# Two-part transformer model: the index scores of the second token tile computed between the two halves of the query projection, and two 64-wide norm rows loaded by another engine

## The chip, the core and the metric

One Trainium2 chip, one core. The metric is the device time of one execution in microseconds (us), taken over several runs. TensorE (PE) multiplies and transposes, VectorE (DVE) and ScalarE (ACT) work on elements, GpSimd (POOL) does a few element operations, SyncE (SP) issues most DMAs.

## The reference

A sequence of 256 tokens with 1024 features passes through two parts. The first part has a sparse-attention layer (layer A), an MLP, a layer with compressed keys and values (layer B) and another MLP. A second part follows. The change is in layer A, which opens the program:

```python
proj = rms_norm(x, a_attn_norm) @ w_in
q = rms_norm(proj[..., :1024].reshape(b, s, 16, 64), q_gain)
k = rms_norm(proj[..., 1024:1088], k_gain)           # one key head
v = proj[..., 1088:1152]
qi, ki, wi = index queries (8 x 64), index key (64), index weights (8)
dots  = einsum('bqhd,bsd->bqhs', qi, ki) * 64 ** -0.5
score = einsum('bqh,bqhs->bqs', wi * 8 ** -0.5, relu(dots))
score = where(admiss, score, NEG)                    # chunks of 64 keys
_, idx = top_k(score, 64)
logits = q @ k[idx] * 64 ** -0.5 + rel_bias[t5_bucket(idx - t)]
h = x + softmax(logits) @ v[idx] @ a_w_o
h = h + relu(rms_norm(h) @ up) ** 2 @ down
```

## The kernel before

Tokens lie in two tiles of 128 partitions (tile 0 and tile 1). Tile 0 sees 128 keys, tile 1 all 256 (`SK`). Everything is fp32 and each product is made of three matmuls: activations and weights are split into a high and a low part. For weights `wsplit` (lines 240 to 263) loads a raw piece through SP (L247, L249), ScalarE writes the high part `whi` (L252, or L260 with a gain), VectorE the low part `wlo` (L255, or L261 with a gain); `mm_tok` (L275, L276, L278) then multiplies. There are 3 raw buffers and 4 buffers of high and low parts. PSUM has 2 `acc` tiles for projections, 2 `tr` for transposes, 3 `lg` for dots and logits, 1 `po` for attention outputs.

A tile scheduler takes the instructions in the order in which the program writes them, models the time of each, and fixes from that one order for each engine. At run time an engine works through its fixed list and never skips an instruction that waits. `keep_in_program_order` (used by `ldk`, L453) pins an instruction where the program writes it. `behind(hold)` asks the scheduler to place what is in it after the instruction `hold`.

Layer A (`layer_a`, from L573) runs so:

- The two halves of tile 0 of `x` are loaded by SP at the head of the program (L146, L148). The attention norm's gain goes to columns. The first key/value/index weights are loaded (L247, four quarters), then tile 1 of `x` (L584). `bcast_row` (L137) loads `gk` and `gq`, the 64-wide key and query norm gains, broadcast to 128 partitions, by DMAs that POOL issues. `norm_x` squares and sums (L175), transposes (L165) and splits the activations into `axh`, `axl`. `gkq` (L593) is the product of the two gains; it is first used when the keys are normed.
- The keys, values, index queries, index keys and index weights come out of two weight chunks of 356 columns (`kvi`).
- `scores(t)` (L630 to L646): four dots on PE (L485, output `lg`), each followed by a ReLU on ACT (L640, `rl`) and two multiply-adds on DVE (L644, `scr`), a chain over 8 index heads.
- `topk(t)` (L648 to L659): eight rounds of MAX (L653) and MATCH_REPLACE (L655) on DVE, a chain too, then the mask `madd` (L658).
- A half `i` of the query projection is a `dense` with `ev_q` (L665 to L675): ACT copies and squares (L668, L669), DVE sums the squares (L671) and computes a factor (L156), POOL scales (L674). `q_T` (L677) transposes the result.
- Attention steps (`att_step`, L533 to L568), two heads each, 16 in all, in a skewed pipeline: `f1` makes logits (L485) and adds the mask `madd` with a matmul by the identity (L487), DVE adds the bias and finds the extremum (L553), ACT takes exponentials (L493); `f2` transposes the probabilities and copies them (L502 on DVE, or ACT); `f3` multiplies with the values (L509). After each four steps `a_done` divides by the sum: `o` (L697) on DVE, then four transposes (L165) and a split into `aoh`, `aol` (L169).
- `out_proj` multiplies with `a_w_o`, whose first two weight chunks are held behind the two masks.

The order of the parts is written out in `PLAN_A` (L28) and played by `weave` (L519): `s` scores, `k` top-k, `q` a half of the query projection, `t10` transposes of tile 1's half 0, `*n` n rounds of the attention pipeline, `**` all that are left.

```python
for f in plan.split():
    if f == "**":
        for _ in rounds: pass
    elif f[0] == "*":
        for _ in range(int(f[1:] or 1)): next(rounds, None)
    else:
        items[f]()
```

Of the kernel before, what the change touches and what calls it, by code (L numbers as in the profile page):

```python
# [24 lines left out]
NACC, NTR, NLG, NPO = 2, 2, 3, 1  # L25


PLAN_A = "s0 k0 q0 q1 t00 t01 s1 * t10 k1 *4 t11 **"  # L28
PLAN_B = "k0 q0 k2 20 q1 k1 30 21 *2 q2 31 * 22 k3 q3 *2 32 *4 23 *2 o00 33 *5 o10 *2 o01 o11"
PLAN_C = "ck mg ms cq q0 mw k0 mn v0 v1 ml B0 *2 q1 *3 B1 *3 o0 k1 *3 k2 * v2 * q2 B2 o1 *2 a0 *2 a1 * b1 * p0 p1 *4 b0 *3"  # L30

# [58 lines left out]
def block_kernel(ctx: ExitStack, tc: tile.TileContext, a, out: bass.AP):  # L90
# [11 lines left out]
    def nm(s):  # L102
        uid[0] += 1
        return f"{s}_{uid[0]}"
# [16 lines left out]
    def sm(s, cols=8):  # L121
        w, n = SMALL.get(s, (8, 2))
        return sp.tile([P, w], F32, tag="s_" + s, name=nm(s), bufs=n)
# [13 lines left out]
    def bcast_row(dst, src_1d, n):  # L137
        G.dma_start(dst, row(src_1d, n))

    def row(src_1d, n):  # L140
        return bass.AP(tensor=src_1d.tensor, offset=src_1d.offset, ap=[[0, P], [1, n]])
# [29 lines left out]
    def rms_stats(h):  # L171
        ss2 = sm("ss2", 2)
        for i in range(2):
            j = tj("sq")
            A.activation(j, h[:, i * 512:(i + 1) * 512], AF.Square, accum_out=ss2[:, i:i + 1])  # L175
        ss = sm("ss", 1)
        V.tensor_tensor(ss[:, :1], ss2[:, 0:1], ss2[:, 1:2], op=OP.add)
        return rsqrt_eps(ss[:, :1], 1.0 / D, 1)

    def norm_T(h, r, gain, x, t):  # L180

        if r is not None or gain is not None:
            hns = t4("hn")
        for i in range(2):
            c = slice(i * 512, (i + 1) * 512)
            hn = h[:, c] if r is None and gain is None else hns[:, c]
            if gain is None:
                if r is not None:
                    V.tensor_scalar(hn, h[:, c], r, None, op0=OP.mult)
            elif r is None:  # L190
                V.tensor_tensor(hn, h[:, c], gain[:, c], op=OP.mult)
            else:
                V.scalar_tensor_tensor(hn, h[:, c], r, gain[:, c], op0=OP.mult, op1=OP.mult)
            ps = transposes(hn, 4)
            put(x, i, t, ps.rearrange("p (k n) -> p k n", k=4))
# [3 lines left out]
    @contextmanager  # L199
    def behind(ins):  # L200

        with ExitStack() as st:
            for i in ins or ():
                st.enter_context(tc.issue_after(i.ins))
            yield

    def norm_x(x, gain, fold=True):


        holds, rs = [tuple(mark[1:])], []  # L210
        for t in range(2):
            if fold:
                rs.append(rms_stats(hres[t]))
                norm_T(hres[t], None, gain, x, t)
            else:
                norm_T(hres[t], rms_stats(hres[t]), gain, x, t)
            holds.append(tuple(mark))
        return holds, rs

    def xpair(s, kt=8):  # L220

        if kt == 2:
            b = t4(s, F32R).rearrange("p (e k n) -> p e k n", e=2, k=2)
            return [b[:, 0]], [b[:, 1]]

        def part(sfx):
            return [t4(s + sfx, F32R, n * 256).rearrange("p (k n) -> p k n", k=n)
                    for n in (min(4, kt - g) for g in range(0, kt, 4))]
        return part("h"), part("l")
# [70 lines left out]
    def out_proj(x, w, scale=None, holds=(None, None)):  # L300
        dense_by_tile([(x, 8, w, 512 * ci, 512, None, lambda t, ps, ci=ci: add_res(t, ci, ps, scale))
                       for ci in range(2)], holds)
# [150 lines left out]
    def ldk(dst, src):  # L453
        tc.keep_in_program_order(nc.sync.dma_start(dst, src))
# [70 lines left out]
    def weave(plan, items, steps):  # L525

        rounds = stages(steps)
        for f in plan.split():
            if f == "**":
                for _ in rounds:  # L530
                    pass
            elif f[0] == "*":
                for _ in range(int(f[1:] or 1)):  # L533
                    next(rounds, None)
            else:
                items[f]()
        assert next(rounds, rounds) is rounds
# [36 lines left out]
    def layer_a():  # L574
# [7 lines left out]
        V.tensor_copy(gcol, gp[:, :8])  # L582
        wkv = [wparts(w, 8, *kvc[0], gain=gcol, by_k=True)]
        nc.sync.dma_start(hres[1], a["x"][0, P:2 * P, :])  # L584
        gk = sm("gk", 64)
        gq = sm("gq", 64)
        bcast_row(gk[:, :64], a["a_k_norm"][0], 64)
        bcast_row(gq[:, :64], a["a_q_norm"][0], 64)
        gkq = sm("gkq", 64)
        x = xpair("ax")  # L590
        holds, rs = norm_x(x, None)
        with behind(holds[2]):
            V.scalar_tensor_tensor(gkq[:, :64], gk[:, :64], 0.125, gq[:, :64], op0=OP.mult, op1=OP.mult)  # L593
        kvi = [t4("kvi") for _ in range(2)]
# [82 lines left out]
        def q_T(t, ci):  # L677
            tp = transposes(qn[t, ci], 4)
            A.activation(qT[t][:, ci * 512:(ci + 1) * 512], tp, AF.Copy)
# [22 lines left out]
        for i in range(2):  # L702
# [3 lines left out]
            for ci in range(2):  # L706
                items["t%d%d" % (i, ci)] = lambda i=i, ci=ci: q_T(i, ci)
        weave(PLAN_A, items, steps)
        out_proj(oT, a["a_w_o"][0], holds=picked)
# [570 lines left out]
    def final():  # L1280
        g = gain_row(a["norm_final_g_2"])
        for t in range(2):
# [7 lines left out]
            for i in range(2):  # L1290
                nc.sync.dma_start(out[0, t * P:(t + 1) * P, i * 512:(i + 1) * 512], gh[i])

    layer_a()
    mlp(0)
    layer_b()
# [30 lines left out]
```

## Time and profile before

| what | value |
|---|---|
| median of 3 runs | 1154.01 us (1153.26 to 1154.15) |
| the profiled execution, its own time | 1153.44 us |
| its span in the trace | 1151.3 us |
| mean granted TensorE clock | 0.998 |
| weights and other data moved | 191.92 MB, mean 167 GB/s |

The span runs from the first to the last recorded instruction. The profiled execution's own time is 2.1 us longer than its span. An engine's busy time is the union of its instructions. The idle time in front of an instruction is given in square brackets with what ended it.

### The profile page before, as it was taken

How to read it: one execution, taken by the hardware profiler on the slowest of the kernel's cores; microseconds unless marked ns; L12 is line 12 of the kernel's file. 1: busy time of each engine (PE TensorE's matmuls, PEld its weight loads, DVE VectorE, ACT ScalarE, POOL GpSimd, SP SyncE). 2: the span in 40 equal slices, each digit the busy share in tenths (PEclk: the TensorE clock that was granted, in tenths of full speed). 3: DMA queues.
4: the chain of work that ended last, by engine and by line, in shares of the span. 5: the costliest groups of instructions: out<-in, count | busy, mean ns of one | idle time of the engine just before them, and what ended most of it. 6: DMA issues, size and time to landing. Idle time of an engine off the chain costs nothing.

```text
span 1151.3 us, 17271 instructions
## 1 busy us (share of the span) xinstructions
PE 1124.7 (98%) x6912; PEld 992.4 (86%) x6912; DVE 678.6 (59%) x1224; ACT 614.1 (53%) x1070; POOL 68.4 (6%) x80
## 2 busy tenths in 40 slices
PE   7989999999998999999999999999999999999997
PEld 6767898889897879989989999888888878999996
DVE  6794754445688574554366976645475566544544
ACT  7654555445487555554446664555554435433443
POOL 1210000000043000000000000010000030000000
PEclk9999999999999999999999999999999999999999
DMA  9540646554462346565538444744544535546641
GB/s 282 199 147 23 216 151 222 182 184 132 132 212 75 104 147 214 170 219 184 171 107 281 147 147 148 240 143 147 183 147 153 183 122 178 206 154 213 202 141 61
DMA packets 105383, 191.92 MB, mean 167 GB/s; under 512 B 6616, under 2 KB 22960, under 8 KB 105304
## 3 DMA queue, kind: packets, MB, share of 16 engines
q1 hardware_dynamic: 104056, 187.16, 48.6%
q0 software_dynamic: 1040, 3.54, 1.0%
q8 instruction: 54, 0.88, 0.3%
q14 instruction: 25, 0.20, 0.1%
q10 hardware_dynamic: 208, 0.13, 0.0%
HBM read 189.68 MB, written 1.13 MB: 166 GB/s over the span
## 4 chain that ended last, share of the span: by engine, by line
PE 92%; DVE 4%; ACT 1%; issue 1%; DMA 0%; POOL 0%; SPq 0%; POOLq 0%; DVEq 0%; ACTq 0%
PE acc L275 10%; PE acc L276 10%; PE acc L278 9%; PE dn L361 7%; PE dn L362 7%; PE dn L364 7%; PE up L310 5%; PE up L313 5%; PE up L311 5%; PE tr L165 3%; PE po L509 2%; PE qk L310 2%; PE qk L311 2%; PE lg L485 2%; PE qk L313 2%; PE fp L310 1%
## 5 line engine op out<-in xcount | busy, mean ns | idle before, releaser
L255 DVE TENSOR_TENSOR wlo<-raw,whi 128x1024 fp32r<-128x1024 f32 (+3 forms) x340 | 385.5, 1177 | 211.3 <-ACT whi L252 211.1
L252 ACT ACTIVATE whi<-raw 128x1024 fp32r<-128x1024 f32 (+3 forms) x340 | 322.9, 1007 | 212.3 <-PE dn L364 86.7
L310 PE MATMUL up<-mxh,whi 128*128 128x256 f32 x448 | 110.9, 281 | 0.0
L311 PE MATMUL up<-mxl,whi 128*128 128x256 f32 x448 | 110.7, 280 | 0.0
L361 PE MATMUL dn<-whi,uh 128*128 128x512 f32 x256 | 100.7, 395 | 0.0
L362 PE MATMUL dn<-wlo,uh 128*128 128x512 f32 x256 | 100.6, 394 | 0.0
L158 POOL TENSOR_TENSOR rr<-rv,mhalf 128x1 f32<-128x1 f32 (+2 forms) x42 | 39.8, 950 | 821.5 <-DVE rv L156 806.2
L310 PEld LDWEIGHTS up<-mxh,whi 128*128 128x128 f32 x448 | 84.3, 188 | 0.7
L311 PEld LDWEIGHTS up<-mxl,whi 128*128 128x128 f32 x448 | 84.2, 188 | 0.7
L275 PE MATMUL acc<-whi,cxh 128*128 128x512 f32 (+1 forms) x192 | 74.5, 389 | 0.0
L276 PE MATMUL acc<-wlo,cxh 128*128 128x512 f32 (+1 forms) x192 | 72.3, 378 | 0.0
L313 PE MATMUL up<-mxh,wlo 128*128 128x256 f32 x448 | 71.0, 280 | 0.0
L364 PE MATMUL dn<-whi,ul 128*128 128x512 f32 x256 | 69.5, 394 | 0.0
L313 PEld LDWEIGHTS up<-mxh,wlo 128*128 128x128 f32 x448 | 60.3, 188 | 0.0
L361 PEld LDWEIGHTS dn<-whi,uh 128*128 128x128 f32 x256 | 48.1, 188 | 13.2 <-ACT whi L252 2.6
L364 PEld LDWEIGHTS dn<-whi,ul 128*128 128x128 f32 x256 | 48.1, 188 | 11.2
L362 PEld LDWEIGHTS dn<-wlo,uh 128*128 128x128 f32 x256 | 48.1, 188 | 10.6
L278 PE MATMUL acc<-whi,cxl 128*128 128x512 f32 (+1 forms) x192 | 50.6, 382 | 0.0
L169 DVE TENSOR_TENSOR ul<-sq,uh 128x512 fp32r<-128x512 f32 x28 | 19.4, 692 | 51.8 <-ACT uh L169 51.5
L310 PE MATMUL qk<-cxh,whi 128*128 128x256 f32 x192 | 49.1, 287 | 0.0
L311 PE MATMUL qk<-cxl,whi 128*128 128x256 f32 x192 | 48.2, 282 | 0.0
L493 ACT ACTIVATE lg<-lg,nx 128x128 f32<-128x128 f32 (+1 forms) x80 | 35.4, 446 | 16.3 <-DVE nx L553 16.3
(414 smaller groups left out, 2410.2 us busy)
## 6 DMA issues: line engine op xcount, KB each, us to landing
raw<-in_w_in SPq DMA_DIRECT2D x38, 1024.0 KB, 5.2
raw<-in_mlp_w_up SPq DMA_DIRECT2D x32, 1024.0 KB, 5.3
raw<-in_mlp_w_down SPq DMA_DIRECT2D x32, 1024.0 KB, 5.1
raw<-in_w_gate SPq DMA_DIRECT2D x10, 1024.0 KB, 5.5
raw<-in_w_up SPq DMA_DIRECT2D x10, 1024.0 KB, 5.1
raw<-in_w_down SPq DMA_DIRECT2D x10, 1024.0 KB, 5.0
raw<-in_w_in SPq DMA_DIRECT2D x6, 688.0 KB
raw<-in_a_w_in SPq DMA_DIRECT2D x4, 1024.0 KB
```

The lines of the kernel that those rows point to most:

```text
L158: G.tensor_tensor(r[:, :n], v[:, :n], mhalf[:, :n], op=OP.pow)
L252: A.activation(hi[:, c], raw[:, c], AF.Copy)
L255: V.tensor_tensor(lo[:, c], raw[:, c], hi[:, c].bitcast(F32), op=OP.subtract)
L275: PE.matmul(o, s0, wh[:, k, :], start=(g + k == 0), stop=False)
L276: PE.matmul(o, s0, wl[:, k, :], start=False, stop=False)
L278: PE.matmul(o, xs(xl, g + k, t), wh[:, k, :], start=False, stop=(g + k == KT - 1))
L310: PE.matmul(o, s0, xh[(g + k) // 4][:, (g + k) % 4, :], start=(g + k == 0), stop=False)
L311: PE.matmul(o, s0, xl[(g + k) // 4][:, (g + k) % 4, :], start=False, stop=False)
L313: PE.matmul(o, wl[:, k, col:col + P], xh[(g + k) // 4][:, (g + k) % 4, :], start=False, stop=(g + k == KT - 1))
L361: PE.matmul(ps, s0, wh[:, k, :], start=(c == 0 and k == 0), stop=False)
L362: PE.matmul(ps, s0, wl[:, k, :], start=False, stop=False)
L364: PE.matmul(ps, xs(u[1], k, t), wh[:, k, :], start=False, stop=(c == nc_ - 1 and k == kt - 1))
```

## The change

Two edits. In `PLAN_A` the item `s1` (scores of tile 1) moves from behind the query transposes `t00 t01` to between `q0` and `q1`. In `layer_a` the rows `gk` and `gq` are allocated and loaded behind `norm_x` instead of ahead of it, and by SP (`ldk`, pinned in program order) instead of POOL (`bcast_row`).

```diff
-PLAN_A = "s0 k0 q0 q1 t00 t01 s1 * t10 k1 *4 t11 **"
+PLAN_A = "s0 k0 q0 s1 q1 t00 t01 * t10 k1 *4 t11 **"
...
         nc.sync.dma_start(hres[1], a["x"][0, P:2 * P, :])
-        gk = sm("gk", 64)
-        gq = sm("gq", 64)
-        bcast_row(gk[:, :64], a["a_k_norm"][0], 64)
-        bcast_row(gq[:, :64], a["a_q_norm"][0], 64)
         gkq = sm("gkq", 64)
         x = xpair("ax")
         holds, rs = norm_x(x, None)
+        gk = sm("gk", 64)
+        gq = sm("gq", 64)
+        ldk(gk[:, :64], row(a["a_k_norm"][0], 64))
+        ldk(gq[:, :64], row(a["a_q_norm"][0], 64))
         with behind(holds[2]):
             V.scalar_tensor_tensor(gkq[:, :64], gk[:, :64], 0.125, gq[:, :64], op0=OP.mult, op1=OP.mult)
```

On SP, at the head of the program, between the load of tile 1 of `x` and the second chunk of key/value weights (`raw_180`):

```order
 L247 DMA raw_105<-in_a_w_in 128x4x356
 L584 DMA h_71<-in_x 128x1024
+L454 DMA gk_173<-in_a_k_norm 128x64
+L454 DMA gq_174<-in_a_q_norm 128x64
 L247 DMA raw_180<-in_a_w_in 128x4x356
 L441 DMA oh_317<-in_c_oh 33x512
```

The two small loads now stand ahead of the second weight chunk on SP; POOL's list loses them.

On VectorE, where tile 0's top-k ends (`scr_389` is tile 0's working array, `scr_390` tile 1's, `rl` a ReLU of two index heads):

```order
 L644 SCALAR_TENSOR_TENSOR scr_389<-rl_421,w_57_351,scr_389 128x128 x2
+L644 SCALAR_TENSOR_TENSOR scr_390<-rl_547,w_66_379,chmask_309 128x256
 L653 MAX m_91_425<-scr_389 128x8
+L644 SCALAR_TENSOR_TENSOR scr_390<-rl_547,w_66_379,scr_390 128x256
 L655 MATCH_REPLACE scr_389<-m_91_425,scr_389 128x128
+L644 SCALAR_TENSOR_TENSOR scr_390<-rl_553,w_66_379,scr_390 128x256
 L653 MAX m_92_428<-scr_389 128x8
+L644 SCALAR_TENSOR_TENSOR scr_390<-rl_553,w_66_379,scr_390 128x256
 L655 MATCH_REPLACE scr_389<-m_92_428,scr_389 128x128
 L653 MAX m_93_431<-scr_389 128x8
```

Four of tile 1's eight score instructions now lie between the first rounds of tile 0's top-k; the other four, and the first round of tile 1's own top-k, lie likewise between tile 0's rounds six to eight.

On VectorE around `o_794`, the attention output of tile 0's first eight heads, in the program before (`scr_390` is in tile 1's top-k, `wlo_1043` and `wlo_1051` are low parts of the output projection's weights):

```order
L655 MATCH_REPLACE scr_390<-m_149_701,scr_390 128x256
L697 TENSOR_TENSOR o_794<-po_740,rl_792 128x512
L653 MAX m_150_704<-scr_390 128x8
L655 MATCH_REPLACE scr_390<-m_150_704,scr_390 128x256
L653 MAX m_151_707<-scr_390 128x8
L169 TENSOR_TENSOR aol_395<-tr_796,aoh_393 128x4x128
L655 MATCH_REPLACE scr_390<-m_151_707,scr_390 128x256
L653 MAX m_152_710<-scr_390 128x8
L655 MATCH_REPLACE scr_390<-m_152_710,scr_390 128x256
L658 TENSOR_SCALAR madd_713<-scr_390 128x256
L255 TENSOR_TENSOR wlo_1043<-raw_1041,whi_1042 128x1024 x2
L255 TENSOR_TENSOR wlo_1051<-raw_1049,whi_1050 128x1024 x2
```

And the same place in the changed program:

```order
L653 MAX m_152_710<-scr_390 128x8
L695 RECIPROCAL rl_864<-l_397 128x8
L655 MATCH_REPLACE scr_390<-m_152_710,scr_390 128x256
L502 COPY pT_788<-tr_785 128x256
L658 TENSOR_SCALAR madd_713<-scr_390 128x256
L255 TENSOR_TENSOR wlo_1043<-raw_1041,whi_1042 128x1024 x2
L255 TENSOR_TENSOR wlo_1051<-raw_1049,whi_1050 128x1024
L697 TENSOR_TENSOR o_794<-po_740,rl_792 128x512
L255 TENSOR_TENSOR wlo_1051<-raw_1049,whi_1050 128x1024
L553 ISA lg_833,nx_400<-lg_834,bias_381 128x256
```

`o_794` stood ahead of the last three rounds of tile 1's top-k; it now stands behind all eight rounds, the mask and three of the four weight splits.

## Rows read from the trace of the kernel before

**Rows 1.** The page, busy time of each engine, with share and number of instructions.

```profile
PE 1124.7 (98%) x6912; PEld 992.4 (86%) x6912; DVE 678.6 (59%) x1224; ACT 614.1 (53%) x1070; POOL 68.4 (6%) x80
```

**Rows 2.** Busy time by stretch: length; PE, PEld, DVE, ACT, POOL; clock, DMA, GB/s.

```profile
55.70:75.70 20.00, 16.32 (x89) 10.94 (x87) 19.57 (x72) 14.45 (x47) 3.42 (x3) 1.00 0.36 131
75.70:101.20 25.50, 25.49 (x138) 19.19 (x138) 18.43 (x55) 11.13 (x40) 0.00 (x0) 1.00 0.25 84
```

**Rows 3.** DVE timeline around `o` of tile 0: start, us, operation, out<-in.

```profile
71.51 0.43 DVE L653 MAX8 m<-scr 128x8 f32<-128x256 f32 x1
...
72.49 0.43 DVE L653 MAX8 m<-scr 128x8 f32<-128x256 f32 x1
...
73.56 0.68 DVE L697 TENSOR_TENSOR o<-po,rl 128x512 f32<-128x512 f32 x1
...
77.78 0.29 DVE L658 TENSOR_SCALAR madd<-scr 128x256 bf16<-128x256 f32 x1
77.99 4.62 DVE L255 TENSOR_TENSOR wlo<-raw,whi 128x1024 fp32r<-128x1024 f32 x4
```

**Rows 4.** PE timeline: first output projection, tile 1's masks, transposes of its `o`.

```profile
75.70 0.50 PE L275 MATMUL acc<-whi,aoh 128*128 128x512 f32 x1
...
79.68 0.82 PE L487 MATMUL lg<-madd,identb 128*128 128x512 bf16 x3
...
102.47 0.66 PE L165 MATMUL tr<-ident,o 128*128 128x128 f32 x4 [1.27 <-DVE ss L177]
```

**Rows 5.** DVE timeline, tile 0's top-k and the weight splits behind it.

```profile
47.73 0.29 DVE L653 MAX8 m<-scr 128x8 f32<-128x128 f32 x1
...
48.45 0.30 DVE L653 MAX8 m<-scr 128x8 f32<-128x128 f32 x1
...
54.51 5.47 DVE L255 TENSOR_TENSOR wlo<-raw,whi 128x1024 fp32r<-128x1024 f32 x4
```

**Rows 6.** DVE timeline, tile 1's scores and the first attention step.

```profile
60.90 0.47 DVE L644 SCALAR_TENSOR_TENSOR scr<-rl,w,scr 128x256 f32<-128x256 f32 x1
61.29 0.27 DVE L553 CUSTOM_DVE_ANT_0 lg<-lg,bias 128x128 f32<-128x128 f32 x1
...
63.99 1.16 DVE L644 SCALAR_TENSOR_TENSOR scr<-rl,w,scr 128x256 f32<-128x256 f32 x1
```

**Rows 7.** POOL timeline, the scaling of the queries.

```profile
47.48 1.11 POOL L674 TENSOR_TENSOR q<-q,rr 128x512 f32<-128x512 f32 x1
...
54.38 1.12 POOL L674 TENSOR_TENSOR q<-q,rr 128x512 f32<-128x512 f32 x1
```

**Rows 8.** Timelines of SP's queue and ACT, the head: loads of tile 0.

```profile
0.74 0.39 SPq L146 DMA_DIRECT2D h<-in_x  x1
...
1.65 0.42 SPq L148 DMA_DIRECT2D h<-in_x  x1
...
3.40 0.63 ACT L175 ACTIVATE sq<-h 128x512 f32<-128x512 f32 x1 [0.74 <-DMA h<-in_x]
...
7.28 0.63 ACT L175 ACTIVATE sq<-h 128x512 f32<-128x512 f32 x1 [3.16 <-DMA h<-in_x]
```

**Rows 9.** DMA queues, first 8 us: packets, MB, share of 16 engines' time.

```profile
q1 hardware_dynamic: 1010, 1.34, 52.4%
...
q0 software_dynamic: 64, 0.07, 12.9%
```

**Rows 10.** Busy time by stretch at the head, columns as in rows 2.

```profile
3.00:6.00 3.00, 1.28 (x5) 0.89 (x5) 0.39 (x2) 0.72 (x2) 0.00 (x0) 1.00 0.72 127
7.00:10.00 3.00, 1.99 (x6) 1.24 (x7) 1.79 (x5) 2.72 (x7) 0.56 (x1) 1.00 1.06 397
```

**Rows 11.** PE timeline, the first projection.

```profile
9.02 0.67 PE L275 MATMUL acc<-whi,axh 128*128 128x356 f32 x1 [0.54 <-ACT whi L260]
...
12.12 0.50 PE L276 MATMUL acc<-wlo,axh 128*128 128x356 f32 x1
...
13.46 0.32 PE L275 MATMUL acc<-whi,axh 128*128 128x356 f32 x1
```

## The prediction

> **What bounds the kernel now.** First the page's busy times: PE is busy 1124.7 of 1151.3 us [rows 1], so PE sets the time, and the change counts by what it does to PE's 27 idle us. Then busy time by stretch, around the first layer's attention [rows 2]: from 55.70 to 75.70 us PE works 16.32 of 20.00 us and DVE 19.57. There DVE is full and PE waits 3.68 us for it. From 75.70 to 101.20 PE works 25.49 of 25.50: work that arrives late at 75.70 is late at 101.20, for nothing there can give. Then the timelines of DVE and PE at the border. DVE alternates between top-k rounds of tile 1 and the attention output `o` of tile 0, which starts at 73.56, ahead of the last three rounds, the mask at 77.78 and the four weight splits at 77.99 [rows 3]. The output projection, which needs it, starts at 75.70 [rows 4], 2.14 us after `o` starts. Last the head of the program, where PE waits for `x`: the second half of tile 0 is issued at 1.65 and used by ACT only at 7.28, after 3.16 us of waiting [rows 8].
>
> **Edit 1, the plan.** It removes no work. Eight multiply-adds of tile 1's scores, so far at 59.9 to 67.5 us among the attention steps, go up between the top-k rounds of tile 0, and tile 1's whole top-k moves ahead with them. The order then puts `o` of tile 0 behind all of tile 1's top-k, the mask and three of four weight splits. An engine works its list off in order, so I price `o` by what newly stands ahead of it on DVE:
>
> - Three rounds: MAX starts at 71.51 and again at 72.49, 0.98 each [rows 3], 2.94 in all. The mask is 0.21 (77.78 to 77.99). Three splits at 4.62/4 = 1.155 are 3.46 [rows 3]. Sum +6.6.
> - Given back by interleaving. A round of 128 columns takes 0.72 when it stands alone (47.73 to 48.45) [rows 5], of which its two instructions' own 0.57 leave gaps that other work can fill; an instruction whose successor needs nothing of it gives way some 0.08 early (a score of 0.47 at 60.90, the next instruction at 61.29) [rows 6]. For eight scores and the top-k rounds around them I take −1.6; the bounds are 0 and −3.2, double.
> - Two slow spots. The four splits at 54.51 take 5.47, 0.85 more than the four at 77.99 [rows 3, 5], while POOL scales queries from 54.38 for 1.12 [rows 7]; a score at 63.99 takes 1.16 where another takes 0.47 [rows 6]. In the new order the first moved score falls beside POOL's product of 47.48 to 48.59 [rows 7] and a later one beside that of 54.38. So this stall stays with other victims: 0, bounds −0.9 and +0.7 (one stall fewer, one more).
>
> So `o` starts some 5.0 us later, at 78.6, and the output projection at 80.7. PE gets part back: tile 1's masks, three 512-wide matmuls that take 0.65 at 79.68 (0.82, less the overlap with the next) [rows 4], are then done in the wait, and the 1.27 us PE idles before the transposes of tile 1's `o` at 102.47 [rows 4] should shrink by some 0.5, since DVE's top-k no longer lies just ahead. 5.0 − 0.65 − 0.5 gives **+3.9**. Bounds: with all of the 3.2 and one stall fewer 6.6 − 3.2 − 0.9 − 0.65 − 0.5 = +1.4; with no interleaving, and one stall more, 6.6 + 0.7 − 0.65 − 0.5 = +6.2. I hold +2.3 to +5.5 as the likely part, since both ends need every item to go one way.
>
> Queued behind `o`: on DVE the fourth split and the attention steps of tile 1, on PE its transposes and all that follow them in its list. The dots on PE and the ReLUs on ACT that move ahead of the second half of the projection are the same number and size; PE does them in a stretch where it never waits, so they cost nothing there and save nothing at their old place, where PE waits anyway. That cover stays.
>
> **Edit 2, the norm rows.** POOL loses two DMAs and SP gets two. They are broadcasts to 128 partitions. In the first 8 us the software queue moves 0.07 MB in 64 packets and takes 12.9% of 16 engines (1.03 us of all sixteen); the hardware queue moves 1.34 MB for 52.4% [rows 9]. Per byte the software one costs about five times as much. And from 3 to 6 us, with the engines busy 0.72, only 127 GB/s arrive; from 7 to 10 us 397 GB/s [rows 10]. Over 3 us that is 0.38 MB where 1.19 would have come, 0.81 MB or 2.0 us at the later rate. The first half of `x` landed 2.66 us after issue (0.74 to 3.40), the second 5.63 (1.65 to 7.28) [rows 8]. Bounds of the gain: 0, if the slowness has another cause, and 2.97, the difference of those two delays. I take **−2.0**, the loss by rate: it lies between the two, and comes from the stretch itself.
>
> Whether PE passes this on: its first projection starts at 9.02 [rows 11], behind the second half of `x`, and it is contiguous from about 13.3 to 61, so all of it moves up, unless weights become late. Against it: SP issues two more loads at 0.4 us each (those of 0.74 and 1.65 took 0.39 and 0.42) [rows 8] ahead of the second weight chunk, +0.8 us on weights whose products start 10 us later, so hidden; if that cover were gone it would cost that 0.8. `gkq` is needed about 18 us, long after either load. POOL's list gets shorter; nothing else queues there early.
>
> **Sum.** +3.9 − 2.0 = +1.9: 1153.44 + 1.9 = 1155.3 for an execution like the profiled one. That one lies 0.57 below the median of 1154.01, so for a median I say **1155.9**. A measurement of this kernel can tell about 0.2%, 2.3 us, from no change.
>
> **Rivals.**
>
> - *The load gains nothing* (B). The slow head would be the sixteen engines' own start, and only the issuer changes. For: two quarter loads of weights are under way then too. Against: 0.07 MB taking 12.9% [rows 9]. Then +3.9, with the 0.8 of issue at worst +4.7: 1157.9 to 1158.7. The Trainium skill, page "DMA: Bandwidth & Descriptors", section "Issuing engines are not separate DMA queues", says that DMAs run on the same sixteen engines whoever issues them and that another issuer saves only its issue time; by it the time would be this rival's. The trace speaks against it only so far as its two queues' cost per byte differs fivefold.
> - *The clock falls in the longer wait* (C). PE would stand idle some 4 us ahead of the late `o`, after a stretch of only 16.32 in 20 [rows 2]. At the head, after idling, 356-column matmuls take 0.67 and 0.50, from 13.46 on 0.32 [rows 11]; the granted clock reads 1.00 (the level of 2.4 GHz) in 7 to 10 all the same [rows 10]. The twelve matmuls from 9.02 to 13.46 take 4.44 us, at half the time each they would take 2.2; losing 2.2 again on top of +1.9 is +4.1, 1158.1. For: PE has waits of 1 to 2 us close together there. Against: no slow matmul follows them now, the one at 75.70 taking 0.50 and its kind behind it less. The Trainium skill, page "TensorE: Matmul & The Clock Gate", section "HAM oscillation — how this bites in real kernels", says that a wait of PE can put it back to half its clock and that the next burst starts cold; whether this wait does, no row here shows.
> - *Faster* (D). DVE, rid of eight scores between 59.9 and 67.5, feeds the attention steps sooner, so PE recovers its 3.68 idle us [rows 2] and `o` is not late: with the load −2.0 − 3.7 = −5.7, 1148.3 at best. For: DVE is the full engine there and gives up about 4 us. Against: the order puts 6.6 us of other work ahead of `o` on that same engine. It decides if `o` starts before about 74.7 (73.56 and the 0.65 + 0.5 that PE gets back, without the head's shift). Between −1.2 and −5.7, middle −3.5: 1150.5.
> - *Part of the lateness is hidden* (E): `o` is only 3.4 later, +2.3 − 2.0 = +0.3, 1154.3.
>
> **Numbers.** Forecast .50 (own range +0.4 to +3.4; .31 of it within 0.2%, .19 above), B .15 and C .12 (slower), D .12 (faster), E .11 (within). So faster .12, same .31 + .11 = .42, slower .19 + .27 = .46. The range leaves out most of D and the worst of B and C with each other: from −1.2 (the upper part of D, near E) to +5.2 (a late `o` at its likely upper end of 5.5, with a load that gains 0.3), 1152.8 to 1159.2.
>
> **What would show it.** Right: the first half's squares at 3.4, the second half's near 5 instead of 7.28, and every PE row of the first 55 us earlier by about 2; `o` of tile 0 near 76.6 on the shifted clock (78.6 − 2.0), with PE's wait before its transposes some 4 us where it was 1.2; tile 1's masks ahead of the first `aoh` matmul, and that near 78.7; the top-k of tile 1 done before 75. B: the second half still at 7. C: `aoh` matmuls above 0.5 us for several us. D: `o` before 73. Wrong altogether would be a second late point: weights of the second chunk waited for between 13 and 20, or PE idle in 80 to 100.

## The result, and the profile after

| | median | lowest to highest | executions |
|---|---|---|---|
| before | 1154.42 us | 1153.26 to 1159.09 | 13 |
| after | 1161.22 us | 1158.42 to 1162.57 | 13 |

The ratio is 1.0053, with a 95% interval of 1.0042 to 1.0064: **slower by 6.8 us** between the medians, by 6.1 us by the ratio. The forecast was 1155.9 in a range of 1152.8 to 1159.2. The sign is that of the forecast's sum; the size is more than three times it, and the range missed.

One thing is needed to read all numbers below. The executions of these kernels fall into two groups, told apart by their time and mostly by the mean granted clock (TensorE's clock as a share of full speed): of 110 executions of the kernel before 63 lie at 1152.8 to 1154.8 us (clock 0.996 to 0.999), 47 at 1155.3 to 1159.9 (0.991 to 0.996). The median before, 1154.42, is the highest of its seven in the lower group. A single execution of `e3_hold` at 1857.86 us and a mean clock of 0.557 is left out of that kernel's numbers.

The profiled execution after took 1162.57 us, the longest of its 13 (span 1160.8, mean clock 0.991 where it was 0.998). Its page answers to [rows 1]:

```profile
PE 1131.9 (98%) x6912; PEld 999.4 (86%) x6912; DVE 676.6 (58%) x1224; ACT 615.0 (53%) x1070; POOL 67.4 (6%) x78
```

The same 6912 matmuls keep PE busy 7.2 us longer: PE does not mainly wait more, it works slower. Where, the windows tell, first of the kernel after (columns as in rows 2; the clock is the third number from the end):

```profile
70.00:80.00 10.00, 5.89 (x34) 4.75 (x34) 9.90 (x28) 4.02 (x17) 0.00 (x0) 0.73 0.40 125
80.00:90.00 10.00, 10.00 (x40) 6.62 (x39) 3.58 (x17) 5.55 (x21) 0.00 (x0) 0.93 0.27 97
...
375.00:380.00 5.00, 2.63 (x11) 1.84 (x10) 3.28 (x10) 3.53 (x13) 0.00 (x0) 0.83 0.98 344
380.00:385.00 5.00, 5.00 (x26) 5.00 (x25) 1.88 (x5) 1.83 (x7) 0.00 (x0) 0.50 0.17 66
385.00:390.00 5.00, 5.00 (x24) 4.39 (x23) 1.12 (x2) 1.06 (x2) 0.00 (x0) 0.65 0.00 0
```

and of the kernel before:

```profile
70.00:80.00 10.00, 8.72 (x56) 6.96 (x55) 9.57 (x28) 3.74 (x13) 0.00 (x0) 1.00 0.01 2
...
365.00:370.00 5.00, 3.52 (x21) 3.24 (x22) 5.00 (x10) 4.39 (x9) 0.14 (x1) 0.83 0.32 105
370.00:375.00 5.00, 3.70 (x18) 2.88 (x17) 3.87 (x10) 2.41 (x10) 0.00 (x0) 0.83 0.93 296
375.00:380.00 5.00, 5.00 (x41) 4.69 (x40) 3.10 (x8) 3.73 (x11) 0.00 (x0) 1.00 0.33 127
```

After, the granted clock falls to half (the level of 1.2 GHz) twice: around 75 to 81, behind the late `o`, and around 378 to 388 in layer B, where no instruction was moved. Before, a low stretch lies in layer B too, but at 368 to 372, where PE waits (3.52 and 3.70 us busy of 5.00) and loses little. After, it lies on back-to-back work.

At the border of the attention, the DVE timeline (columns as in rows 3) of the kernel after, to be held against [rows 3]:

```profile
71.34 0.43 DVE L653 MAX8 m<-scr 128x8 f32<-128x256 f32 x1
...
72.54 0.28 DVE L658 TENSOR_SCALAR madd<-scr 128x256 bf16<-128x256 f32 x1
72.74 3.49 DVE L255 TENSOR_TENSOR wlo<-raw,whi 128x1024 fp32r<-128x1024 f32 x3
76.14 0.68 DVE L697 TENSOR_TENSOR o<-po,rl 128x512 f32<-128x512 f32 x1
```

`o` comes at 76.14, where it came at 73.56, behind the mask and three splits. PE's timeline there:

```profile
72.87 0.81 PE L487 MATMUL lg<-madd,identb 128*128 128x512 bf16 x3 [0.35 <-DVE madd L658]
76.97 1.09 PE L165 MATMUL tr<-ident,o 128*128 128x128 f32 x4 [3.29 <-DVE o L697]
...
78.99 0.77 PE L275 MATMUL acc<-whi,aoh 128*128 128x512 f32 x1
79.57 0.63 PE L276 MATMUL acc<-wlo,aoh 128*128 128x512 f32 x1
...
81.54 0.40 PE L275 MATMUL acc<-whi,aoh 128*128 128x512 f32 x1
...
105.83 0.66 PE L165 MATMUL tr<-ident,o 128*128 128x128 f32 x4 [1.21 <-DVE rv L156]
```

PE waits 3.29 us, then its output projection runs at 0.63 a matmul until 81.54 and at 0.40 behind that. The masks (72.87) lie ahead of it, as forecast, and the wait before the transposes of tile 1's `o`, 1.27 in [rows 4], is 1.21.

At the head, ACT's timeline shows the second half of tile 0 used at 4.80 instead of 7.28 [rows 8]:

```profile
3.37 0.63 ACT L175 ACTIVATE sq<-h 128x512 f32<-128x512 f32 x1 [0.71 <-DMA h<-in_x]
...
4.80 0.63 ACT L175 ACTIVATE sq<-h 128x512 f32<-128x512 f32 x1 [0.71 <-DMA h<-in_x]
```

POOL's software queue is gone from the first 8 us, and the stretch from 3 to 6 brings 299 GB/s (columns as in rows 2), where [rows 10] show 127:

```profile
3.00:6.00 3.00, 2.34 (x9) 1.60 (x9) 0.71 (x4) 1.93 (x5) 0.02 (x1) 1.00 0.96 299
```

The edit moved the two loads in time too. POOL issued the first at 1.25, beside the halves of `x`; SP issues it at 5.04, when the second half is already in use (timelines, before and after):

```profile
1.25 0.70 POOL L138 DMA_DIRECT2D gk<-in_a_k_norm  x1 [0.81 <-POOLq L1322]
```

```profile
5.04 0.43 SPq L454 DMA_DIRECT2D gk<-in_a_k_norm  x1
```

The first projection starts at 6.70 instead of 9.02 [rows 11], but its matmuls only reach 0.32 at 13.75, where they did at 13.46 before:

```profile
6.70 0.66 PE L275 MATMUL acc<-whi,axh 128*128 128x356 f32 x1 [0.70 <-ACT whi L260]
...
11.16 0.50 PE L275 MATMUL acc<-whi,axh 128*128 128x356 f32 x1
...
13.50 0.41 PE L276 MATMUL acc<-wlo,axh 128*128 128x356 f32 x1
13.75 0.32 PE L275 MATMUL acc<-whi,axh 128*128 128x356 f32 x1
```

The lead in us (after minus before) of the same instruction: −2.3 at the first projection, −0.5 at the first index dots (38.74 before, 38.23 after), +3.3 at the first `aoh` matmul, +3.8 late in the first MLP, +4.3 at 339 where layer B begins, +8.7 behind layer B, +8.1 at 550, +9.1 at the end of this pair of profiled executions. In layer B and behind it PE's list is the same in both.

### The profile page after: what moved, and what is told of

Its sections match the earlier page's. It is cut to its first block, busy times and chain, and to the rows that moved or that the text cites. A ratio compares the mean times of both kernels' runs of the same rounds, so it can differ in the third digit from the quotient of the medians.

```text
span 1160.8 us, 17261 instructions
## 1 busy us (share of the span) xinstructions
PE 1131.9 (98%) x6912; PEld 999.4 (86%) x6912; DVE 676.6 (58%) x1224; ACT 615.0 (53%) x1070; POOL 67.4 (6%) x78
## 4 chain that ended last, share of the span: by engine, by line
PE 89%; DVE 5%; DMA 2%; ACT 2%; issue 1%; SPq 0%; POOL 0%; POOLq 0%; ACTq 0%
PE acc L275 9%; PE acc L276 9%; PE acc L278 9%; PE dn L361 7%; PE dn L364 7%; PE dn L362 7%; PE up L313 5%; PE up L310 5%; PE up L311 5%; PE tr L165 3%; PE po L509 2%; PE qk L311 2%; PE qk L313 2%; PE qk L310 2%; PE lg L485 2%; DVE wlo L255 2%
```

## Experiments

The texts quoted were written before each run and name the theories that they set against each other. All ratios are to runs of the kernel before on the same chip; "before" is its median there. `e1` to `e4`, `e5` to `e8`, `e9` to `e12` and the last two ran on four different chips.

**Each edit alone.** `e1_load` has the old `PLAN_A` and the new loads, `e2_plan` the new `PLAN_A` and the old loads.

> Only the loads of the two norm rows move to SP; the plan is the old one. Theory 1 (the two edits are independent; the head gains 2.3 us, as the first projection's start at 6.70 instead of 9.02 showed, and nothing gives it back): 1152 us. Theory 2 (a stretch of low TensorE clock in layer B near 370 us is cheap only where the old program happens to have it, in PE's idle time; anything that shifts the program moves it onto work): 1152 plus up to 4.5, the layer-B stretch 340 to 400 us showing another place or length of the low clock.

> Only the plan changes; the norm rows are loaded as before. Theory 1 (the late attention output costs 3.3 us of waiting net of the head's gain, so 5 to 6 us in all, and a stretch at low clock behind the wait 1.4): 1160 to 1163.5 us, the first half of tile 0's output at 78.4, PE idle over 3 us ahead of its transposes. Theory 2 (the lateness itself is small and the rest is the low clock in layer B): 1157 or less when that stretch falls on idle time.

Measured: `e1_load` 1155.16 us (1152.91 to 1158.23, 12 executions; before 1154.19), ratio 0.9996 (0.998 to 1.0012); six executions at 1152.9 to 1154.6 and six at 1155.7 to 1158.2. `e2_plan` 1162.21 us (1160.62 to 1163.02), ratio 1.005 (1.0031 to 1.0069). The plan alone carries the whole loss; its PE waits 3.29 us for `o`, until 78.43, and the clock falls in both places. What the loads bring drowns in the two groups of executions.

**What stands ahead of `o`.** `e3_hold` keeps the change and asks the scheduler to place the second chunk's weight splits behind `o`:

```diff
-            V.tensor_tensor(o..., op=OP.mult)
+            done_o.append(V.tensor_tensor(o..., op=OP.mult))
...
-        out_proj(oT, a["a_w_o"][0], holds=picked)
+        out_proj(oT, a["a_w_o"][0], holds=(picked[0], picked[1] + done_o[:1]))
```

`e4_split` leaves the splits and moves tile 1's last three top-k rounds and its mask behind `o` instead (`k1` plays five rounds, a new item `f1` the other three under `behind(done_o[:1])`).

> The changed kernel with one edit: the output projection's second weight chunk is also held behind the first attention output, so on VectorE the output stands ahead of all four splits, still behind the whole top-k and the mask. Theory 1: the output starts at 72.7 instead of 76.1, PE's wait of 3.29 before its transposes goes, and with it the low clock from 77 to 81: 1161.2 - 3.4 - 1.4 = 1156.4 us. Rival (the splits were not what it waited for, or PE then waits for the splits themselves): 1159 to 1161.

> The changed kernel with tile 1's top-k cut in two: the last three rounds and the mask are issued behind the first attention output, which then stands where it stood before the change, ahead of three rounds, the mask and the splits. Theory 1: the output starts near 70, PE loses its long wait, and the head's 2.3 us are kept: 1151 to 1153 us, faster than before. Rival (PE then waits for the mask of tile 1 or for the splits instead): 1156 or more, with a new wait between 75 and 90 us.

Measured: `e3_hold` 1153.04 us (11 executions), ratio 0.9989 (0.9971 to 1.0007), in two groups, 6 executions at 1151.9 to 1153.0 and 5 at 1156.1 to 1157.8: the median lies at the upper edge of the lower one. `e4_split` 1157.92 us, ratio 1.0001 (0.9984 to 1.0019), 4 at 1153.4 to 1154.3 and 8 at 1157.4 to 1158.8. In `e3_hold` the 3.29 us wait is gone and with it the low clock, as PE's timeline shows:

```profile
73.42 0.81 PE L487 MATMUL lg<-madd,identb 128*128 128x512 bf16 x3 [0.32 <-DVE madd L658]
74.12 0.63 PE L165 MATMUL tr<-ident,o 128*128 128x128 f32 x4
...
75.44 0.50 PE L275 MATMUL acc<-whi,aoh 128*128 128x512 f32 x1
75.78 0.39 PE L276 MATMUL acc<-wlo,aoh 128*128 128x512 f32 x1
...
76.93 0.39 PE L275 MATMUL acc<-whi,aoh 128*128 128x512 f32 x1
```

`o` starts at 73.29 in `e3_hold` and at 72.42 (expected near 70) in `e4_split`, and the first MLP's first product follows at 120.84 and 120.99 (before 122.17, after 125.50). So the loss in layer A is the lateness of `o`, and taking the three splits from ahead of it is enough to undo it. The moved scores themselves cost nothing that can be measured.

**Layer B's clock.** Twenty-three extra transposes of the identity, whose results nothing uses, fill PE's waits in layer B; nothing else is touched. `e5_fill_before` does it to the kernel before, `e6_fill_after` to the changed one, `e7_fill_hold` to `e3_hold`.

```diff
+WARM_B = {(2, 0, 0): 20, (1, 0, 1): 3}
...
-        ps = transposes(p, n)
+        ps = trp("tr")
+        for i in range(warm):
+            PE.transpose(ps[:, i % 4 * P:(i % 4 + 1) * P], ident, ident)
+        ps = transposes(p, n, ps)
```

> The kernel before with 23 extra transposes of the identity on PE in layer B (20 ahead of one pair of transposes of probabilities near 372 us, 3 ahead of another near 366), written into the tile that the real transposes then overwrite; nothing else moves. They fill waits that PE has there. Theory 1 (executions differ by a stretch of low TensorE clock that follows PE's sparse work near 365 to 377 us; 11 of 30 executions of the kernel before take 1156.6 to 1159.0, the others 1153.3 to 1154.8): no execution above 1155.5, granted clock 0.997 or more in all. Rival (the scatter comes from elsewhere): the same two groups, all later by up to 0.5 us.

> The changed kernel with the same 23 extra transposes in layer B. Theory 1 (of the 6.8 us that the change cost, 3.3 are the late attention output, 1 to 1.5 the low clock behind that wait, and the rest low clock in layer B): 1157.5 to 1158.8 us in all executions, against 1161.2; the layer-B stretch at granted clock 1.00, that of 70 to 90 us still below. Rival (layer B's loss is not the clock's): 1160.5 to 1162.

> Experiment e3 (the output ahead of all four weight splits) with the same 23 extra transposes in layer B. Theory 1: all executions as e3's lower group, 1152 to 1153 us, clock 0.998, so faster than before by 1.2 to 2.5. Rival: two groups as in e3 (1152 to 1153 and 1156 to 1158).

Measured, all in one comparison (before 1156.38, 26 executions of both groups): `e5_fill_before` 1154.44 us (1153.6 to 1155.09), ratio 0.9975 (0.9964 to 0.9987); `e6_fill_after` 1157.82 us (1157.03 to 1160.38), 1.0016 (1.0004 to 1.0028); `e7_fill_hold` **1153.1 us** (1152.57 to 1153.91), 0.9965 (0.9953 to 0.9977). In `e6_fill_after` the clock in layer B is whole and that behind `o` is still low:

```profile
70.00:80.00 10.00, 5.88 (x34) 4.84 (x34) 9.90 (x27) 3.99 (x17) 0.00 (x0) 0.85 0.39 131
...
375.00:380.00 5.00, 4.45 (x37) 4.35 (x38) 3.36 (x12) 3.46 (x13) 0.00 (x0) 1.00 1.00 358
380.00:385.00 5.00, 5.00 (x38) 4.49 (x38) 2.06 (x5) 2.69 (x7) 0.00 (x0) 1.00 0.04 12
```

The upper group vanishes in all three but for one execution of `e6_fill_after` (1160.38, clock 0.994). Layer B's clock costs the changed kernel 1161.22 − 1157.82 = 3.4 us between medians; in the two profiled executions, after against `e6_fill_after`, the lead grows by 4.4 us in layer B (from 0.6 to 5.0) and nowhere else by more than 0.5. The rest of the change costs 1157.82 − 1154.44 = 3.4 us.

**The loads without that noise.** `e9_load_fill` is `e1_load` with the same filling. `e8_late_rows` is `e3_hold` with the two norm rows loaded behind the second key/value chunk instead of ahead of it:

```diff
+        kvi = [t4("kvi") for _ in range(2)]
+        wkv.append(wparts(w, 8, *kvc[1], gain=gcol))
...
         ldk(gk[:, :64], row(a["a_k_norm"][0], 64))
         ldk(gq[:, :64], row(a["a_q_norm"][0], 64))
...
-        kvi = [t4("kvi") for _ in range(2)]
-        wkv.append(wparts(w, 8, *kvc[1], gain=gcol))
```

> Experiment e1 (the loads alone, the old plan) with the 23 extra transposes in layer B, to be read beside e5 (the kernel before with the same transposes, 1154.44). Theory 1 (the loads start the first projection 2 us sooner, but TensorE runs at half its clock until about 13.5 us either way, so that only some 0.9 us are left at the index dots near 38 us): 1153.3 to 1153.9. Theory 2 (nothing is left): 1154.2 to 1154.8. Theory 3 (the forecast's term): 1152.4.

> Experiment e3 with the two norm rows loaded by SP behind the second chunk of key/value weights instead of ahead of it. Theory 1 (the head gained 2.3 us at PE's first projection and lost it by 24 us because the second chunk's loads, issued at 6.28 behind the two small ones, landed late): the chunk issued near 5.1, its first high part at 13.9 or before instead of 14.88, the fourth of the key/value outputs near 30 instead of 30.83, and the fastest executions 0.5 to 1 us below e3's 1151.9. Theory 2 (from 10 to 38 us the stream of weights, or ACT which splits them, sets the pace whatever the issue order): the fourth output at 30.3 to 31, the time as e3's.

Measured: `e9_load_fill` 1153.36 us (1152.92 to 1153.85, 12 executions), against 1154.44 of `e5_fill_before` (1153.6 to 1155.09; on another chip, but the two hardly overlap): the loads are worth **−1.1 us**. The traces agree: the first index dots start at 38.74 to 39.72 in the four profiled kernels with the old loads (mean 39.34) and at 38.06 to 38.74 in the ten others with the new ones and an unchanged head (mean 38.50), 0.8 apart. `e8_late_rows` 1157.85 us (1153.81 to 1160.75), ratio 1.0007 (0.9992 to 1.0022). Ten of its 12 executions lie in the upper group, though its `o` isn't late. Its chunk is issued 1.2 us earlier than in `e3_hold` (5.04 for 6.28) and ACT makes its high part at 13.06 instead of 14.88, but then ACT waits for PE for 3.09 us, until 21.83, and the fourth key/value output comes at 31.16 (`e3_hold`: 30.83). What is late there is not the load; the 0.8 us of issue in front of the chunk is hidden, as forecast.

**PE kept working at the head.** `e12_head_warm` is `e7_fill_hold` with ten products of a zeroed tile ahead of the first transposes, used by nothing:

```diff
+    warm = cp.tile([P, P], F32, name="warm")
+    V.memset(warm, 0.0)
+    ps = trp("tr")
+    for i in range(10):
+        PE.matmul(ps[:, i % 4 * P:(i % 4 + 1) * P], warm, warm, start=True, stop=True)
```

> Experiment e7 with ten products of a zeroed tile on PE at the very start, ahead of the first transposes. Theory 1 (the clock rises only after PE has worked for a while, and the 2.3 us that the loads gain at the first projection are lost because it rises near 13.5 us either way): matmuls of 0.32 us before 12 us, the first index dots 0.5 to 1 us earlier than e7's 38.68, and 1152 to 1152.8 us against e7's 1153.1. Rival (weights and ScalarE set the pace to 38 us): faster matmuls, but the index dots at 38.4 to 39 and no gain.

Measured: 1152.98 us (1152.56 to 1156.08), ratio 0.9988 (0.9975 to 1.0001). PE's timeline at the head:

```profile
1.05 4.63 PE L155 MATMUL tr<-warm 128*128 128x128 f32 x20 [1.05 <-DVE warm L152]
...
8.34 0.43 PE L282 MATMUL acc<-whi,axh 128*128 128x356 f32 x1 [1.21 <-ACT axh L176]
8.61 0.33 PE L283 MATMUL acc<-wlo,axh 128*128 128x356 f32 x1
```

The matmuls are at 0.33 from 8.61 on instead of from 13.75, though the projection starts 1.6 us later than after. The first index dots come at 38.11, 0.57 ahead of `e7_fill_hold`, and the first MLP's product at 120.19, 0.64 ahead; other executions with the same loads and no such products have the dots at 38.06 to 38.74, and the median moves by 0.1, which isn't told from nothing. (The scheduler also reordered a few instructions.)

**The price of the low clock in layer A.** `e10_warm_a` is `e6_fill_after` with three logits products and five repeated mask products moved into PE's wait for `o`.

> The changed kernel with the 23 extra transposes in layer B and, in layer A, tile 1's first three logits products and five repeated mask products moved into PE's wait for the late attention output, which stays behind all four weight splits (1.2 us later than in the changed kernel). Theory 1 (the slow output products at 77 to 81 us come from TensorE's low clock after a long wait): products at 0.40 from the first on, granted clock 1.00 in 70 to 90 us, and 1157 to 1158 us in spite of the later output. Rival (they are slow for another reason): 0.6 us each as before, and 1158.5 to 1159.5.

Measured: 1158.14 us (1157.02 to 1159.29), ratio 1.003 (1.0015 to 1.0045), no better than `e6_fill_after`. The `aoh` matmuls do run at 0.40, but now the masks and logits ahead of them are slow, behind two waits of 0.94 and 1.41 us further ahead:

```profile
68.97 0.41 PE L167 MATMUL tr<-ident,lg 128*128 128x128 f32 x2 [0.94 <-DVE rl L702]
...
72.08 0.69 PE L167 MATMUL tr<-ident,lg 128*128 128x128 f32 x2 [1.41 <-ACT pT L507]
...
74.17 1.91 PE L489 MATMUL lg<-KT,qT 128*128 128x512 f32 x2
```

In this execution the low clock moved and was not removed, and `o` itself is 1.7 us later than after (77.82), so the price isn't settled. The executions give a hint: two with a mean clock of 0.998 and 0.999 took 1157.0 and 1157.2, four with 0.995 took 1158.0 to 1159.3.

**Is it the shift alone?** `e11_delay` gives the kernel before 36 unused transposes at the end of layer A, so that layer B starts 3.4 us late with nothing else changed. `e13_after_d32` and `e14_after_d48` give 32 and 48 to the changed kernel.

```diff
-            tp = transposes(o, 4)...
+            ps = trp("tr")
+            for i in range(36 if (t, half) == (1, 1) else 0):
+                PE.transpose(ps[:, i % 4 * P:(i % 4 + 1) * P], ident, ident)
+            tp = transposes(o, 4, ps)...
```

> The kernel before with 36 extra transposes of the identity at the end of layer A's attention, so that all that follows comes 3 to 3.5 us later, with no other change and nothing in layer B. Theory 1 (whether the low clock in layer B falls on work is a matter of the single execution): two groups again, about 1156.5 to 1158 and 1160 to 1162.5, in about equal parts. Theory 2 (a shift by some 3 us as such puts the low clock onto work): nearly all executions at 1160 to 1162.5.

> The changed kernel with 32 extra transposes of the identity at the end of layer A's attention: everything behind comes some 2.5 to 3 us later, the low clock at 77 to 81 us stays where it is. Theory 1 (a stretch of low clock in layer A sets when the next one can begin in layer B, so the share of executions that lose there depends on the distance between the two): another share than the changed kernel's 11 of 13, some executions at 1160 to 1161 (1157.8 and the shift). Theory 2 (whoever has the long wait in layer A loses in layer B, at any distance): nearly all executions at 1163 to 1165.5. Theory 3 (chance of the single execution): about half of them.

> The same with 48 extra transposes: some 4.3 to 5 us later. Theory 1: again another share, lower group near 1162.5, upper near 1166.5. Theory 2: nearly all executions at 1165 to 1167.5. Theory 3: about half of them.

Measured: `e11_delay` 1156.39 us (1155.59 to 1161.67), ratio 1.0029 (1.0013 to 1.0045), seven at 1155.6 to 1156.6 and four at 1159.0 to 1161.7. Starting layer B late is not enough to bring the low clock onto its work every time. `e13_after_d32` 1162.91 us (1160.67 to 1164.46), 1.0069 (1.005 to 1.0087); `e14_after_d48` 1165.62 us (1164.23 to 1166.98), 1.0094 (1.0076 to 1.0113). By the mean clock, three executions of `e13_after_d32` lie at 1160.7 to 1162.3 (0.995) and three at 1163.5 to 1164.5 (0.992); of `e14_after_d48` one lies at 1164.2 and five at 1165.3 to 1167.0. Six each are too few to tell the theories apart. The profiled execution of `e13_after_d32` (1164.46 us) tells something else. Its layer B runs at 1.00 throughout, and the low clock lies at 107 to 114:

```profile
105.00:110.00 5.00, 3.79 (x22) 3.65 (x21) 2.72 (x7) 1.64 (x4) 0.57 (x1) 0.69 0.00 0
110.00:115.00 5.00, 5.00 (x16) 4.01 (x17) 0.00 (x0) 0.00 (x0) 0.00 (x0) 0.63 0.00 0
...
380.00:385.00 5.00, 2.58 (x16) 2.02 (x16) 4.74 (x11) 2.19 (x9) 0.00 (x0) 1.00 0.78 242
```

and PE's timeline of it shows what was slow there:

```profile
106.86 1.11 PE L165 MATMUL tr<-ident,o 128*128 128x128 f32 x4 [1.21 <-DVE rv L156]
...
113.73 0.40 PE L275 MATMUL acc<-whi,aoh 128*128 128x512 f32 x1
```

Up to 120 us PE and DVE have the same list there as in the kernel after, and PE waits the same 1.21 us ahead of the same transposes, which are done in 0.66 after and take 1.11 here. The same program, the same wait: once the clock falls and once it doesn't.

## Why the prediction was wrong

**The step that failed** is the weighing of rival C, the clock. The forecast gave its sum no term for the clock ("no slow matmul follows them now"), and C a chance of .12 and a price of 2.2 us, at the wait for `o` alone. It fell in all six profiled executions of the changed plan that have a late `o`, and it cost more than C's price, in two places:

- *Behind `o`*, 1.8 us. The transposes to the first `aoh` take 78.99 − 76.97 = 2.02 where `e3_hold` takes 75.44 − 74.12 = 1.32, 0.70 more; the first six `aoh` matmuls take 81.54 − 78.99 = 2.55 where `e3_hold` takes 1.49, 1.06 more. In the profiled `e6_fill_after` the low stretch is shorter (0.85 in 70 to 80, for 0.73) and the same two sums give 1.3. C's 2.2 was near. The Trainium skill, page "TensorE: Matmul & The Clock Gate", section "HAM oscillation — how this bites in real kernels", says that a wait of PE can put it back to half its clock, so that the next burst starts cold; here the trace agrees, with 3.29 us of waiting and 0.63 a matmul behind it.
- *In layer B*, 3.4 us (`e6_fill_after`), some 270 us behind the last place where PE's order changed (111 us). No rival had this. The kernel before showed the low stretch at 365 to 375 already, at a clock of 0.83 in two windows, but the rows read for the forecast lay only around the change.

**The plan's other terms.** `o` came at 76.14 (forecast 76.6), `aoh` at 78.99 (78.7), masks first and tile 1's top-k done before 75, as said; rival D, for which `o` had to come by about 74.7, fell with that. But that `o` and `aoh` came where they were forecast is luck: two terms were off against each other. Counted from the first index dots, `o` is 3.1 us later (37.91 behind them, before 34.82), not 5.0, and the head's lead is 0.5 there in this pair, not 2.0. For the lateness alone rival E, with its 3.4, had the better size. The DVE groups in that stretch of 37.91 us show where the 1.9 went (group, busy and mean, idle before):

```profile
L255 DVE TENSOR_TENSOR wlo<-raw,whi 128x1024 fp32r<-128x1024 f32 x7 | 8.1, 1217 | 0.0
...
L644 DVE SCALAR_TENSOR_TENSOR scr<-rl,w,chmask 128x128 f32<-128x128 f32 (+1 forms) x2 | 1.6, 809 | 0.4 <-ACT rl L640 0.4
```

and the last group before:

```profile
L644 DVE SCALAR_TENSOR_TENSOR scr<-rl,w,chmask 128x128 f32<-128x128 f32 (+1 forms) x2 | 0.8, 412 | 0.4 <-ACT rl L640 0.4
```

and the same stretch as one window, before and after:

```profile
38.74:73.56 34.82, 32.04 (x152) 23.36 (x150) 29.92 (x106) 25.55 (x63) 11.63 (x9) 1.00 0.41 140
```

```profile
38.23:76.14 37.91, 32.63 (x155) 23.66 (x153) 33.73 (x119) 25.67 (x63) 11.86 (x9) 0.98 0.40 133
```

Seven splits take 8.1 us where the four of [rows 5] took 5.5: three more add 2.6, not 3.46, for the stall of 0.85 there is gone, while the first moved score takes 0.8 more (1.6 for the two `chmask` scores, 0.8 before). The groups' sums rise by 5.3 us, DVE's busy time by 33.73 − 29.92 = 3.8: 1.5 is overlap of neighbours, where the forecast took 1.6 for interleaving. The rest is idle time, 4.90 before and 4.18 after, which the sum left out.

PE's return was 1.07 us by the first MLP's product where the clock holds (`e3_hold`: 45.40 us from `aoh` to it, before 46.47), near the 0.65 + 0.5 of the forecast; in the kernel after the clock eats it (46.51). Not in the sum either: the first MLP takes 0.7 us longer in every profiled kernel with the new plan (first product to its last `r`: 164.78 before, 165.47 after), and the second MLP gives 0.6 of it back (the lead falls from 8.7 to 8.1). PE is full throughout the first in both (109.00 of 109.00 us from 131 on before, 109.60 of 109.60 from 134.4 on after), and in two of their three lines the `up` matmuls have a median of 282 ns where it was 280. The cause is open.

**The load term** had the right sign and was mis-sized: −1.1 us for −2.0. The first projection gained 2.3 us in this pair, near the 2.0 that the rates gave; what failed is "all of it moves up". Matmuls there take 0.50 to 0.67 until about 13.5, whether PE began at 9.02 or 6.70, and the lead of the same matmul is 2.30 at 11.16 (13.46 before), 1.23 at 13.50 (14.73), 0.91 at 18.36 (19.27) and 0.53 at 24.93 (25.46). So 1.1 of it goes while the matmuls are slow, the rest in short waits behind. That faster matmuls would keep it is not shown: `e12_head_warm` has them and gains 0.6 in its trace, within the scatter of the head. Rival B (nothing gained) fell: the second half of tile 0 is used at 4.80, not at 7. That the software queue is the cause is argued, not shown: the loads also went from 1.25 to 5.04, out of the way of `x`, and no run has them on SP early or on POOL late. So no run here sets the issuer's own part against the rule that another issuer saves only its issue time (the Trainium skill, page "DMA: Bandwidth & Descriptors", section "Issuing engines are not separate DMA queues"); what the traces show is the rate from 3 to 6 us, 127 GB/s with POOL's early loads and 299 without.

**The account.** Without layer B's low clock: `e9_load_fill` − `e5_fill_before` = −1.1 for the loads; `e6_fill_after` − `e9_load_fill` = +4.5 for the plan with a late `o`, 1.8 of it the clock behind `o`. With +3.4 for layer B that makes 6.8. So the plan without any clock costs +2.7 (+3.2 with the 1.3 of `e6_fill_after`'s own trace), within the +2.3 to +5.5 held likely, and the loads and plan together +1.6 (+2.1), near the +1.9 of the sum. Part of that is luck. Where the +3.9 was priced, at the end of layer A, the first MLP's product is 125.50 − 122.17 = 3.33 us later; with the head's lead of 0.51 and without the clock's 1.76 that is 2.1. The rest came in the first MLP and in later layers, where the forecast had nothing. The numbers come from different comparisons, and the intervals of their ratios are some 1 to 1.4 us to either side, so the split is sure to one or two microseconds.

**Open.** Why kernels with a late `o` lie in the upper group in nearly every execution (after 11 of 13, by time, `e2_plan` all 7) and others in about half (before 47 of 110, `e1_load` 6 of 12, `e3_hold` 5 of 11, `e4_split` 8 of 12) is not settled, nor whether the late `o` is what matters: `e8_late_rows`, whose `o` isn't late, has 10 of 12, on a chip where the kernel before has 17 of 26. A constant shift of layer B did not decide it (`e11_delay`, 4 of 11), and in `e13_after_d32` the low clock lies at another wait, at 107 to 114. What decides it in a single execution is not shown.

**The version that beats both** is `e7_fill_hold`, 1153.1 us, ratio 0.9965: the change, the second chunk's splits behind `o`, and layer B's waits filled. Most of that is the upper group gone: against the lower group of the kernel before in the same comparison (nine executions, median 1153.77) 0.7 us are left. And the new plan has little part in it: `e9_load_fill`, with the old plan, reaches 1153.36.

## What to carry to other kernels

When a scheduler may fill a gap with work nobody waits for, look at what it puts ahead of the one result that the bounding engine needs, and hold that work behind it: here three weight splits made `o` 3.3 us late (37.91 us behind the index dots, 34.60 in `e3_hold`) and one line took it back. Price a longer wait of TensorE with the clock behind it, and read the granted clock over the whole program, not just around the change: half clock costs little where PE waits anyway (368 to 372 before) and 3.4 us where it falls on full work. Where a kernel's executions fall into two groups, remove that first (a few unused matmuls in the waits), and small edits become measurable.

## What the hardware showed that I had not expected

- The same waits were followed by half clock in one execution and not in another. In layer B PE waits 0.8, 0.7 and 2.3 us with work in between and is busy 2.63 of 5 us in one window both of `e3_hold`, where the clock stays at 1.00, and of the kernel after, where it falls to 0.50. The windows and PE's longest wait of `e3_hold`:

```profile
370.00:375.00 5.00, 2.63 (x19) 2.10 (x19) 3.94 (x11) 3.36 (x13) 0.00 (x0) 1.00 0.93 322
375.00:380.00 5.00, 5.00 (x38) 4.48 (x38) 2.46 (x7) 2.89 (x9) 0.00 (x0) 1.00 0.23 88
```

```profile
372.84 0.77 PE L165 MATMUL tr<-ident,p 128*128 128x128 f32 x2 [2.25 <-ACT p L493]
```

  PE's timeline there in the kernel after:

```profile
377.67 0.79 PE L165 MATMUL tr<-ident,p 128*128 128x128 f32 x2 [2.26 <-ACT p L493]
378.27 1.89 PE L867 MATMUL lg<-KTb,QT 98*128 98x256 f32 x4
379.95 3.52 PE L509 MATMUL po<-kvb,pT 128*128 128x64 f32 x16
```

  The sixteen `po` matmuls take 3.52 us; before, at 375.15, the same sixteen took 1.90.
- The granted clock reads 1.00 from the first microseconds [rows 10], though the same 356-column matmul takes 0.50 there and 0.32 later. Ten products of zeros from 1.05 us on brought 0.33 at 8.61. So at the head the durations have to be read; the column doesn't show it.
- Two loads of 64 floats broadcast to 128 partitions held up the half tile of `x` beside them by 2.5 us (7.28 to 4.80) when POOL issued them at 1.25 and 1.94, and not when SP issued them at 5.04 and 5.52. Whether the issuer or the time made the difference is not separated.
